# Past gates' sums at the down projection, a fixed order for TensorE in the mixer, prompt attention in rounds

## Chip, core and metric

The kernel runs on one core of a Trainium2 chip. The metric is the device time of one execution in microseconds (us). Engines: TensorE (PE; its weight loads are PEld), VectorE (DVE), ScalarE (ACT), GpSimd (POOL) and SyncE (SP). SP computes nothing here; it issues most DMAs, POOL issues the others, among them all indirect ones (gathers by an index).

## The reference

One step of a hybrid decoder layer, for a prompt of 1024 tokens and 8 samples of 4 new tokens, each with 2048 past tokens in pages of 128.

```
x = x + 0.5 * SwiGLU_1(RMSNorm(x))            # "up 1", "down 1"
p = RMSNorm(x) @ w_in                         # q | k | v | forget gates | B | C | u   ("mixer")
s[t,j] = q_t.k_j / 8 + sum of log f over (j,t]   # prompt, causal, 8 heads of 64
sample: the same over 16 gathered pages of k, v and log f, then the 4 new tokens
conv   = B * conv3(C * u)                     # 512 channels
x = x + w_out @ concat(RMSNorm(attn), RMSNorm(conv))
x = x + 0.5 * SwiGLU_2(RMSNorm(x));  final RMSNorm
suffix = lax.cumsum(lp, axis=1, reverse=True) - lp    # lp: the past log f, from the pages
```

All is float32. Each product of the projections is made of three matmuls (L102 to L104): weight and operand are split into a high part (a cast on ACT, L85 for weights, L191 for operands) and a remainder (a subtraction on DVE, L87 and L192).

## The kernel before

The 1056 tokens lie along the free axis, in four chunks of 264 for the feed-forward parts and in three of 352 for the mixer. The program is one stream of stages. For PE, ACT and DVE a scheduler sets the order within a stage; each engine then takes its instructions strictly in that order, and so do the queues of SP and POOL. A DMA is issued when its place in the queue has come and what it waits for is there.

**Up 1** (0 to about 480 us of the span) makes h = silu(.) * (.), and POOL stores it to h_d (L325, L330). **Down 1** (to about 747 us) takes h back: SP loads pieces of 128x528 (`h<-h_d`, L383), ACT and DVE split them (L191, L192), PE multiplies them with w2a (`ps<-h`). Eleven pieces are one chunk of tokens.

**Mixer** (to about 1160 us). First come the gates' logits and the first q tiles (`forget`, `proj`), then all of k, v, q and the convolution, 352 columns at a time (`pg<-XH`). Between them the samples' attention is dealt out as a generator A, 0.27 steps for each product: `sample_keys` gathers a page chunk `kvraw` (1 MB: two direct loads by SP, two gathers by POOL) and multiplies it (`sc`, L832), `sample_values` the same with v (`pv`, L880). What the past gates add comes from `load_gates`: 16 gathers of 64 KB (`R`, L598) for each group of four samples, which four scans on DVE (L823) sum into S. The indices `idl` are put in place by 16 small moves on SP (`by_pair`, L461). Weights of the mixer (`wraw<-in_w_in`) are loaded by SP too, in the same queue as the page chunks.

**Prompt attention** (1173 to 1327 us), 64 blocks of 128 queries, head by head. `logits` makes S (L1074, L1075, L1077), its maximum on DVE (L1079), the exponential on ACT (L1082), the sum's reciprocal and a scaling on DVE (L1083, L1084). `flip` transposes the probabilities (`ptp`, L1093) and copies them to PT (L1096); `weigh` makes O for two blocks at once (L1107), whose two halves ACT and DVE copy to `at`. `load_qk` (L1063) brings a head's KA, KB, QA, QB by eight loads on SP, `load_v` a pair's v. Two norms of the convolution's output (`conv_norm`: squares L140, `pco` L141, root L168, reciprocal L169, scaling L188, parts L191 and L192) are put after blocks 20 and 44. The order is set by `LA`, `PVD` and the scheduler:

```
LA, PVD, PTB, PRB = 3, 2, 5, 4
CONV_AT = (20, 44)
```

Then **w_out** (from 1327 us), **up 2** and **down 2**.

Of the kernel before, what the change touches and what calls it, by code (L numbers as in the profile page):

```python
# [8 lines left out]
F32 = mybir.dt.float32  # L9
# [9 lines left out]
P = 128  # L19
# [20 lines left out]
LA, PVD, PTB, PRB = 3, 2, 5, 4  # L40
RA = 0.27
CONV_AT = (20, 44)
# [384 lines left out]
def kernel(ctx: ExitStack, tc: tile.TileContext, io: dict):  # L427
# [34 lines left out]


# [8 lines left out]
    at_d = [dp.tile([P, TOK], F32, name=f"at_d{t}") for t in range(NHP)]  # L472
    qx_d = dp.tile([H, 4, SEQ], F32, name="qx_d")
# [64 lines left out]

    es_x = ExitStack()
    xpool = pool(es_x, "xh", "right")  # L540
    XH = xpool.tile([P, KD, TOK], F32R, name="XH")
# [26 lines left out]

    with ExitStack() as es:
        smp = pool(es, "smp", "left")  # L570
        mix = pool(es, "mix", "left")
# [4 lines left out]


        pt = mix.tile([P, NB * PAGES], I32, name="pt")
        nc.sync.dma_start(pt, io["pt"].rearrange("b s -> (b s)").rearrange("(o n) -> o n", o=1)
                          .broadcast_to([P, NB * PAGES]))  # L580
        ptl = mix.tile([P, 2, PAGES], I32, name="ptl")
        for b in range(NB):
            nc.sync.dma_start(ptl[32 * (b % 4):32 * (b % 4) + 32, b // 4, :],
                              io["pt"][b:b + 1, :].broadcast_to([32, PAGES]))
        cin = mix.tile([P, 2], I32, name="cin")
        nc.sync.dma_start(cin, io["cin"])
        idx = mix.tile([P, NB * PAGES], I32, name="idx")
        nc.vector.tensor_scalar(idx, pt, P, None, ALU.mult)
        nc.vector.tensor_tensor(idx, idx, cin[:, 0:1].broadcast_to([P, NB * PAGES]), ALU.add)
        ido = mix.tile([P, 2, PAGES], I32, name="ido")  # L590
        nc.vector.tensor_scalar(ido, ptl, H, None, ALU.mult)
        nc.vector.tensor_tensor(ido.rearrange("p g s -> p (g s)"), ido.rearrange("p g s -> p (g s)"),
                                cin[:, 1:2].broadcast_to([P, 2 * PAGES]), ALU.add)
        idl = mix.tile([P, 2, PAGES], I32, name="idl")
        by_pair(idl, lambda r: ido[r:r + 8])

        def gather(dst, src, ix):
            nc.gpsimd.indirect_dma_start(out=dst, out_offset=None, in_=src,  # L598
                                         in_offset=bass.IndirectOffsetOnAxis(ap=ix, axis=0))
# [189 lines left out]
        keys, new = [], []  # L789
# [9 lines left out]
        gates = {}  # L799

        def load_gates(g):

            gates[g] = []
            for i in range(4):
                R = smp.tile([P, 4, P], F32, tag="R", bufs=4, name="R")
                for s in range(4):
                    col = PAGES - 1 - (4 * i + s)
                    gather(R[:, s, :], io["lf"], idl[:, g, col:col + 1])
                gates[g].append(R)

# [5 lines left out]
        def sample_keys(g):  # L816

# [3 lines left out]
            for i, R in enumerate(gates[g]):  # L821
                n = 512 if i < 3 else 511
                nc.vector.tensor_tensor_scan(S[:, 512 * i + 1:512 * i + 1 + n],  # L823
                                             ones[:, 0:1].broadcast_to([P, n]),
                                             R.rearrange("p s k -> p (s k)")[:, :n],
                                             S[:, 512 * i:512 * i + 1], ALU.mult, ALU.add)
            for j in range(4):
                ps = psc.tile([P, 512], F32, tag="sc", name="sc")
                for b4 in range(4):
                    raw = kv_chunk()  # L830
                    for hp in range(NHP):
                        nc.tensor.matmul(ps[quarter(hp)], QZ[:, g, hp, 32 * b4:32 * b4 + 32],  # L832
                                         raw[:, :, hp * P:hp * P + P], start=b4 == 0, stop=b4 == 3)
                    if b4 < 3:
                        yield
                ks = slice(512 * j, 512 * j + 512)
                nc.vector.scalar_tensor_tensor(S[:, ks], ps, cq[:, g:g + 1], S[:, ks], ALU.add, ALU.add)
                yield
            pn = ptr.tile([P, 512], F32, tag="tr", name="pn")[:, :NS]
            if g == 0:  # L840
                load_gates(1)
            while not keys:
                yield
# [12 lines left out]
            yield  # L856
            PT = PTs[g] = smp.tile([P, PAGES + 1, P], F32, tag="PT", bufs=2, name="PT")
            for s0 in range(0, PAGES + 1, 4):
                n = min(4, PAGES + 1 - s0)
# [4 lines left out]
                if s0 == 4:  # L864
                    yield
            yield

        def sample_values(g):
            PT = PTs[g]
            while not new:  # L870
                yield

            pv = ppv.tile([P, 512], F32, tag="pv", name="pv")
            for b4 in range(4):
                cs = slice(P * b4, P * b4 + P)
                for j in range(4):
                    raw = kv_chunk()
                    for s in range(4):
                        for hp in range(NHP):
                            nc.tensor.matmul(pv[quarter(hp), cs], PT[:, 4 * j + s, quarter(hp)],  # L880
                                             raw[:, s, hp * P:hp * P + P], start=j == 0 and s == 0, stop=False)
                    if j < 3:
                        yield
                for hp in range(NHP):
                    nc.tensor.matmul(pv[quarter(hp), cs], PT[:, PAGES, quarter(hp)],
                                     new[0][:, hp * P:hp * P + P], start=False, stop=True)
                yield
            M = smp.tile([P, 512], F32, tag="M", bufs=1, name="M")
            nc.scalar.activation(M, pv, AF.Copy, scale=sums[g])
            po = ptr.tile([P, 512], F32, tag="tr", name="po")  # L890
# [9 lines left out]


        def vnew():
# [4 lines left out]
            new.append(VS)  # L907
# [51 lines left out]
        def values():  # L959
# [12 lines left out]
            vnew()  # L972
# [5 lines left out]
        def k_proj():  # L978
            for t in range(NHP):
                yield from proj(NHP + t, "k", t)  # L980
            keys.append(True)

        def q_rest():
            for t in range(1, NHP):
                yield from proj(t, "q", t, range(NMC - 1))

# [5 lines left out]
        load_gates(0)  # L992
# [3 lines left out]
        take(q0, 8)  # L996
        next(gate)
        take(q0, 5)
        next(gate)
        for t in range(1, NHP):  # L1000
            take(proj(t, "q", t, (NMC - 1,)), 5)
            next(gate, None)
# [17 lines left out]
    with ExitStack() as es:  # L1020
        ap_ = pool(es, "ap", "left")
        mix = pool(es, "mixb", "left")
        pco = pool(es, "pco", space=PSUM)
# [3 lines left out]
        RX = HD + 4  # L1027
        K.tmp = ap_
# [12 lines left out]
        def load_v(hp):  # L1041
            vt = ap_.tile([P, SEQ], F32, tag="vt", bufs=1, name="vt")
            nc.sync.dma_start(vt, v_d[hp])
            V = ap_.tile([P, 8, P], F32, tag="V", bufs=2, name="V")
            for j0 in range(0, 8, 4):
                pt_ = ptr.tile([P, 512], F32, tag="tr", bufs=2, name="ptv")
# [5 lines left out]

        def load_qk(h):

            hp, pr = h // 2, slice(HD * (h % 2), HD * (h % 2) + HD)
            KA, KB, QA, QB = (ap_.tile([P, SEQ], F32R, tag=n, bufs=2, name=n)
                              for n in ("KA", "KB", "QA", "QB"))
            (qh, ql), (kh, kl) = qk_d["q", hp], qk_d["k", hp]
            for dst, src in ((KA[:HD], kh[pr, :]), (KA[HD:], kh[pr, :]),
                             (QA[:HD], qh[pr, :]), (QA[HD:], ql[pr, :]),  # L1060
                             (KB[:HD], kl[pr, :]), (KB[HD:RX], kx_d[h]),
                             (QB[:HD], qh[pr, :]), (QB[HD:RX], qx_d[h])):
                nc.sync.dma_start(dst.bitcast(F32), src)  # L1063
            return KA, KB, QA, QB
# [285 lines left out]
```

## Time and profile before

| | us |
|---|---|
| median of 3 runs (lowest, highest) | 2198.26 (2195.49, 2204.02) |
| the profiled execution, its own time | 2176.51 |
| its span | 2174.8 |
| PE busy | 2082.3 |
| DVE busy | 1344.5 |
| ACT busy | 874.5 |
| POOL busy | 265.8 |

A span is the time from the first to the last instruction. The profiled execution is 1% under the median. Times in us, of one instruction in ns. PEclk is the granted clock of PE as a share of 2.4 GHz; 0.5 is its lower level, 1.2 GHz, and a mean between the two means that a stretch had some of both. A row of the timeline gives an instruction's start and duration, and in brackets how long its engine was idle before it and what ended that. `SPq` and `POOLq` are the engines' queues, in which the instructions that issue DMAs stand.

### The profile page before, as it was taken

Reading aid. Unit: us, or ns where it says so; the run is one execution under the profiler, and the core shown is the slowest. Engines: PE = TensorE matmul, PEld = TensorE weight load, DVE = VectorE, ACT = ScalarE, POOL = GpSimd, SP = SyncE. Lnnn points to the kernel's source line nnn. Section 1 sums busy time; section 2 is a strip of 40 time slices with the busy share of each in tenths; the row PEclk is TensorE's granted clock in tenths of the full one; section 3 lists DMA queues with packets and bytes.
Section 4 is the critical chain, followed back from the end, with each engine's and each line's share of the span. In section 5 each row is a group of like instructions: output and inputs, shape, how many; then the busy total and the mean of one; then the engine's idle time right before and its main releaser. Section 6 shows DMA issues by size and latency. Waiting matters only on the chain.

```text
span 2174.8 us, 44542 instructions
## 1 busy us (share of the span) xinstructions
PE 2082.3 (96%) x17570; PEld 1987.5 (91%) x17570; DVE 1344.5 (62%) x2586; ACT 874.5 (40%) x1738; POOL 265.8 (12%) x367
## 2 busy tenths in 40 slices
PE   7999999999999968899997999999999999999998
PEld 7999999999999856689996777989999999999997
DVE  8877777776656641132223785897667677775354
ACT  6533333345434421222112775454333333464343
POOL 0010011100000065323430000000110100100000
PEclk9999999999999988999997999999999999999999
DMA  6222223257545468887985545332222222496354
GB/s 210 79 96 84 84 87 98 85 178 237 178 154 203 157 183 271 305 289 234 281 255 149 125 102 166 133 114 84 89 77 72 86 87 84 136 321 202 108 177 132
DMA packets 139234, 336.84 MB, mean 155 GB/s; under 512 B 28192, under 2 KB 47616, under 8 KB 137488
## 3 DMA queue, kind: packets, MB, share of 16 engines
q1 hardware_dynamic: 117168, 265.23, 39.1%
q0 software_dynamic: 21856, 68.76, 9.0%
q8 instruction: 138, 2.26, 0.4%
q14 instruction: 72, 0.59, 0.1%
HBM read 277.66 MB, written 56.24 MB: 154 GB/s over the span
## 4 chain that ended last, share of the span: by engine, by line
PE 90%; DMA 4%; DVE 2%; ACT 1%; issue 1%; SPq 1%; POOL 1%; DVEq 0%; ACTq 0%; POOLq 0%
PE ps L104 23%; PE ps L103 23%; PE ps L102 23%; PE pg L102 4%; PE pg L103 4%; PE pg L104 4%; PE O L1107 2%; PE ptp L1093 1%; PE pv L880 1%; DMA wraw<-in_w_in 1%; PE sc L832 1%; PE S L1074 1%; PE ps L141 1%; PE S L1075 1%; DMA wraw<-in_w_out 1%
## 5 line engine op out<-in xcount | busy, mean ns | idle before, releaser
L104 PE MATMUL ps<-op,wl 128*128 128x264 f32 x2604 | 742.8, 286 | 0.0
L103 PE MATMUL ps<-op,wh 128*128 128x264 f32 x2604 | 741.1, 285 | 0.0
L102 PE MATMUL ps<-op,wh 128*128 128x264 f32 x2604 | 739.7, 285 | 1.3 <-ACT wh L85 0.9
L85 ACT CAST wh<-wraw 128x512 fp32r<-128x512 f32 x542 | 317.3, 600 | 497.2 <-PE ps L103 283.1
L87 DVE TENSOR_TENSOR wl<-wraw,wh 128x512 fp32r<-128x512 f32 x542 | 350.5, 662 | 232.5 <-ACT wh L85 208.0
L102 PEld LDWEIGHTS ps<-op,wh 128*128 128x128 f32 x2604 | 490.6, 189 | 2.1 <-ACT wh L85 1.1
L103 PEld LDWEIGHTS ps<-op,wh 128*128 128x128 f32 x2604 | 489.4, 188 | 0.5 <-DVE op L192 0.2
L104 PEld LDWEIGHTS ps<-op,wl 128*128 128x128 f32 x2604 | 489.6, 188 | 0.2
L102 PE MATMUL ps<-h,wh 128*128 128x264 f32 x1408 | 402.4, 286 | 0.0
L104 PE MATMUL ps<-h,wl 128*128 128x264 f32 x1408 | 398.7, 283 | 2.6 <-DVE wl L87 2.6
L103 PE MATMUL ps<-h,wh 128*128 128x264 f32 x1408 | 400.9, 285 | 0.0
L104 PEld LDWEIGHTS ps<-h,wl 128*128 128x128 f32 x1408 | 265.5, 189 | 2.8 <-DVE wl L87 2.8
L102 PEld LDWEIGHTS ps<-h,wh 128*128 128x128 f32 x1408 | 265.4, 188 | 0.2
L103 PEld LDWEIGHTS ps<-h,wh 128*128 128x128 f32 x1408 | 265.3, 188 | 0.2
L102 PE MATMUL pg<-XH,wh 128*128 128x352 f32 x576 | 193.0, 335 | 8.4 <-ACT wh L85 7.6
L103 PE MATMUL pg<-XL,wh 128*128 128x352 f32 x576 | 189.2, 329 | 0.0
L104 PE MATMUL pg<-XH,wl 128*128 128x352 f32 x576 | 187.7, 327 | 0.0
L85 ACT CAST wh<-s 128x512 fp32r<-128x512 f32 x176 | 108.1, 616 | 121.7 <-PE ps L103 110.4
L87 DVE TENSOR_TENSOR wl<-s,wh 128x512 fp32r<-128x512 f32 x176 | 120.5, 689 | 25.2 <-ACT wh L85 20.5
L102 PEld LDWEIGHTS pg<-XH,wh 128*128 128x128 f32 x576 | 110.9, 193 | 27.0 <-issue 13.2
L325 POOL DMA_DIRECT2D h_d<-t x79 | 42.6, 540 | 601.9 <-DVE t L324 601.9
L104 PEld LDWEIGHTS pg<-XH,wl 128*128 128x128 f32 x576 | 110.1, 191 | 0.9 <-DVE sm L854 0.8
(266 smaller groups left out, 2548.0 us busy)
## 6 DMA issues: line engine op xcount, KB each, us to landing
wraw<-in_w2a SPq DMA_DIRECT2D x48, 512.0 KB
wraw<-in_w2b SPq DMA_DIRECT2D x48, 512.0 KB
h_d<-t POOLq DMA_DIRECT2D x176, 132.0 KB, 2.0
h<-h_d SPq DMA_DIRECT2D x88, 264.0 KB
kvraw<-in_kc SPq DMA_DIRECT2D x64, 256.0 KB
kvraw<-in_vc SPq DMA_DIRECT2D x64, 256.0 KB
wraw<-in_w1a SPq DMA_DIRECT2D x28, 512.0 KB
wraw<-in_w3a SPq DMA_DIRECT2D x28, 512.0 KB
```

What stands on the lines that cost most here:

```text
L85: nc.scalar.copy(wh, x)
L87: nc.vector.tensor_sub(wl, x, wh)
L102: nc.tensor.matmul(ps, w[0], x[0], start=start, stop=False)
L103: nc.tensor.matmul(ps, w[0], x[1], start=False, stop=False)
L104: nc.tensor.matmul(ps, w[1], x[0], start=False, stop=stop)
L141: nc.tensor.matmul(ps, self.ones, sq, start=n == 0, stop=n == len(xs) - 1)
L325: nc.gpsimd.dma_start(h_d[2 * p + 1][:, f, :], t)
L832: nc.tensor.matmul(ps[quarter(hp)], QZ[:, g, hp, 32 * b4:32 * b4 + 32], raw[:, :, hp * P:hp * P + P], start=b4 == 0, stop=b4 == 3)
L880: nc.tensor.matmul(pv[quarter(hp), cs], PT[:, 4 * j + s, quarter(hp)], raw[:, s, hp * P:hp * P + P], start=j == 0 and s == 0, stop=False)
L1074: nc.tensor.matmul(S[:, k0:k1], QA[:, qs], KA[:, k0:k1], start=True, stop=False)
L1075: nc.tensor.matmul(S[:, k0:k1], QB[:RX, qs], KB[:RX, k0:k1], start=False, stop=not last)
L1107: nc.tensor.matmul(O[HD * b + q:HD * b + q + 32], V[:, j, c0 + q:c0 + q + 32], pt[:, j, :], start=j == 0, stop=j == n)
```

## The change

Four things change together.

1. **The past gates' sums** leave the mixer. The page indices, the 32 gathers R and the eight scans (now into a buffer B) are written between up 1 and down 1, and eight stores put the sums into a new tensor `bs_d` in memory. The mixer loads S from there (`new_sums`).
2. **TensorE's order in the mixer** is fixed by hand. The samples' work is a list of steps, `key_pages`, `new_keys`, `turn`, `value_pages`, `keep`, that `sample` deals out at a rate RA = 0.265 between the products. There are six page buffers instead of five, and five chunks are fetched while the gates' logits are made.
3. **Prompt attention in rounds.** A round is two blocks. For each round PE makes S of the next round, the transposes of this one and O of the one before, in an order fixed by hand. Both convolution norms stand after round 9; the transposing tiles have three PSUM buffers instead of two, shared with `pco`.
4. **Operands on POOL's queue.** `load_qk`, v and the stores of `at` are issued by POOL; the first head's operands already when the samples' steps are used up, during the last products of the convolution.

```diff
-LA, PVD, PTB, PRB = 3, 2, 5, 4
-RA = 0.27
-CONV_AT = (20, 44)
+RX = HD + 4
+PTB, PRB = 4, 4
+RA = 0.265
+CONV_AT = 9
...
     es_l.close()
     es_r.close()
+    es_x = ExitStack()
     xpool = pool(es_x, "xh", "right")
+    pt = xpool.tile([P, NB * PAGES], I32, name="pt")
+    idx = xpool.tile([P, NB * PAGES], I32, name="idx")
+    with ExitStack() as es:
+        gp = pool(es, "gp", "left")
...
+        idl = gp.tile([P, 2, PAGES], I32, name="idl")
+        by_pair(idl, lambda r: ido[r:r + 8])
+        for g in range(2):
+            last = None
+            for i in range(4):
+                R = gp.tile([P, 4, P], F32, tag="R", bufs=2, name="R")
+                for s in range(4):
+                    col = PAGES - 1 - (4 * i + s)
+                    gather(R[:, s, :], io["lf"], idl[:, g, col:col + 1])
+                B = gp.tile([P, 512], F32, tag="B", bufs=2, name="B")
+                nc.vector.tensor_tensor_scan(B, ones[:, 0:1].broadcast_to([P, 512]),
+                                             R.rearrange("p s k -> p (s k)"),
+                                             last if i else 0.0, ALU.mult, ALU.add)
+                last = B[:, 511:512]
+                n = 512 if i < 3 else 511
+                nc.sync.dma_start(bs_d[g][:, 512 * i + 1:512 * i + 1 + n], B[:, :n])
...
-            raw = smp.tile([P, 4, 512], F32, tag="kvraw", bufs=5, name="kvraw")
+            raw = smp.tile([P, 4, 512], F32, tag="kvraw", bufs=6, name="kvraw")
...
-            while len(raws) < min(n + 4, len(chunks)):
+            while len(raws) < min(n + 6, len(chunks)):
...
+        def new_sums(g):
             S = smp.tile([P, PAST + P], F32, tag="S", bufs=1, name="S")
             nc.gpsimd.memset(S[:, PAST + NS:], NEG)
             nc.vector.memset(S[:, 0:1], 0.0)
...
+            nc.sync.dma_start(S[:, 1:PAST], bs_d[g][:, 1:PAST])
+            Ss[g] = S
...
-        load_gates(0)
         gate = forget()
         q0 = proj(0, "q", 0)
         next(gate)
         take(q0, 8)
+        fetch()
...
-        A = chain(sample_keys(0), sample_keys(1), sample_values(0), sample_values(1))
-        due = 0.0
-        for _ in chain(k_proj(), values(), q_rest(), conv(range(4))):
-            due += RA
-            if due >= 2:
-                take(A, 2)
-                due -= 2
-        for _ in A:
-            pass
+        work = chain(k_proj(), values(), q_rest(), conv(range(4)))
+        for n, _ in enumerate(work):
+            sample(2 * int(RA * n / 2))
+            if not steps:
+                break
+        es_s.close()
+        es_a = ExitStack()
+        ap_ = pool(es_a, "ap", "left")
+        qk = {0: load_qk(0)}
+        for n, _ in enumerate(work):
+            if n == 5:
+                keep(1)
...
-                nc.sync.dma_start(dst.bitcast(F32), src)
+                nc.gpsimd.dma_start(dst.bitcast(F32), src)
...
-                copy = nc.vector.tensor_copy if h % 2 and j0 else nc.scalar.copy
+                copy = nc.vector.tensor_copy if i % 2 and j0 else nc.scalar.copy
...
-            nc.sync.dma_start(at_d[h // 2][vc, 256 * m:256 * m + 256], at[vc])
+            nc.gpsimd.dma_start(at_d[h // 2][vc, 256 * m:256 * m + 256], at[vc])
...
+        front(0)
+        for r in range(len(rounds)):
+            front(r + 1)
+            middle(r)
+            back(r - 1)
+            if r == CONV_AT:
+                for c in range(NCH // 2):
+                    conv_norm(c, K.tmp.tile([P, 4, CH], F32, tag="co", bufs=1, name="co"),
+                              ptr.tile([P, 512], F32, tag="tr", bufs=3, name="pco")[:, :CH])
+        back(len(rounds) - 1)
```

In `front(r)` the two calls of `logits` are made, for the first round of a head `load_qk` of the next head, and for every second head the load of v; `middle(r)` flips both blocks and turns v; `back(r)` calls `weigh`.

Three places show how the instructions move (line numbers after the change are one more up to the new code, so L383 is L384). The first is SP's queue where up 1 ends and down 1 begins; `in_w2a` are weights of down 1, `h` its operand. Before:

```order
L77 DMA wraw<-in_w3a 128x1024
L77 DMA wraw<-in_w2a 128x1024 x2
L77 DMA wraw<-in_w2a 128x768
L383 DMA h<-h_d_81 128x528 x11
L77 DMA wraw<-in_w2a 128x1024 x2
L77 DMA wraw<-in_w2a 128x768
```

and after the change, behind the same first weights and the moves of the page indices:

```order
L802 ISA x2
L582 DMA bs_d_117<-B 128x512 x3
L582 DMA bs_d_117<-B 128x511
L582 DMA bs_d_118<-B 128x512 x3
L582 DMA bs_d_118<-B 128x511
L384 DMA h<-h_d_81 128x528 x11
L593 DMA x<-in_xT 128x2112
L78 DMA wraw<-in_w2a 128x1024 x2
```

The eleven loads of h stand behind the eight stores of the sums. The second place is DVE at the same point; `s`, `u`, `m` and `t` are the gate products of up 1. Before:

```order
L307 TENSOR_TENSOR s_6244<-ps,m_6229 128x264
L192 TENSOR_TENSOR h<-h 128x528
L87 TENSOR_TENSOR wl<-wraw,wh 128x512
L311 TENSOR_TENSOR u_6260<-ps,m_6229 128x264
L192 TENSOR_TENSOR h<-h 128x528
L87 TENSOR_TENSOR wl<-wraw,wh 128x512
L192 TENSOR_TENSOR h<-h 128x528
```

and after, where L577 is the scan and R what POOL gathers:

```order
L330 TENSOR_TENSOR t<-t,s_6246 128x264
L561 TENSOR_SCALAR idx<-pt 128x128
L562 ISA idx<-cin,idx 128x256
L577 SCALAR_TENSOR_TENSOR B<-ones,R 128x512
L577 SCALAR_TENSOR_TENSOR B<-ones,B,R 128x512 x3
L577 SCALAR_TENSOR_TENSOR B<-ones,R 128x512
L577 SCALAR_TENSOR_TENSOR B<-ones,B,R 128x512 x3
L193 TENSOR_TENSOR h<-h 128x528 x11
```

The splitting of h stands behind the scans; PE's order at this place is the same in both. The third place is PE in the attention where the convolution's squares are summed. Before, such rows stand among others, here one by itself:

```order
L1048 MATMUL ptv<-cst,vt 128x128 x8
L1093 MATMUL ptp<-cst,Pr 128x128
L141 MATMUL pco<-sq,ones 128x264
L1093 MATMUL ptp<-cst,Pr 128x128 x5
L1074 MATMUL S<-KA,QA 128x512
```

and after:

```order
L1131 MATMUL ptp<-cst,Pr 128x128 x7
L1145 MATMUL O<-PT,V 32x128 x6
L142 MATMUL pco<-sq,ones 128x264 x8
L1112 MATMUL S<-KA,QA 128x512
L1113 MATMUL S<-KB,QB 128x512
```

The eight matmuls of both norms now follow one another.

## Rows read from the trace of the kernel before

**Rows 1.** The page: busy time of each engine.

```profile
PE 2082.3 (96%) x17570; PEld 1987.5 (91%) x17570; DVE 1344.5 (62%) x2586; ACT 874.5 (40%) x1738; POOL 265.8 (12%) x367
```

**Rows 2.** Stretches: us, busy PE PEld DVE ACT POOL, PEclk, DMA share, GB/s.

```profile
480.00:500.00 20.00, 20.00 (x167) 20.00 (x166) 14.49 (x28) 10.17 (x21) 1.08 (x2) 1.00 0.97 345
792.00:832.00 40.00, 18.35 (x91) 10.12 (x90) 6.52 (x9) 3.01 (x6) 30.52 (x33) 0.66 0.72 234
832.00:870.00 38.00, 33.37 (x195) 27.54 (x194) 6.90 (x13) 8.38 (x18) 15.04 (x16) 0.91 0.84 282
870.00:908.00 38.00, 31.50 (x191) 22.95 (x193) 8.47 (x14) 6.81 (x13) 12.65 (x15) 0.91 0.85 276
950.00:1000.00 50.00, 50.00 (x336) 40.95 (x336) 12.58 (x19) 9.27 (x18) 21.11 (x22) 1.00 0.94 322
1174.00:1190.00 16.00, 13.13 (x58) 9.81 (x58) 7.14 (x17) 7.52 (x21) 0.00 (x0) 0.54 0.69 176
1173.00:1327.00 154.00, 142.53 (x1748) 108.58 (x1749) 111.67 (x252) 107.48 (x265) 0.00 (x0) 0.94 0.45 108
```

**Rows 3.** Chain of waits, mixer's front: start, us, what.

```profile
813.26 5.23 DMA R<-in_lf,idl
...
840.15 8.86 DMA wraw<-in_w_in
```

**Rows 4.** Waits of PE ahead of the attention: total, times, longest.

```profile
PE S L1074 <- DMA QA<-q_d: 13.0, 1, 13.0
```

**Rows 5.** Chain of waits after the attention.

```profile
1335.43 6.06 DMA wraw<-in_w_out
...
1359.10 3.52 DMA wraw<-in_w_out
```

**Rows 6.** Timeline of SP, ACT, DVE and POOL where down 1 begins.

```profile
461.06 15.47 SPq L383 DMA_DIRECT2D h<-h_d  x11
...
471.94 0.63 ACT L191 CAST h<-h 128x528 fp32r<-128x528 f32 x1
...
473.15 0.70 DVE L192 TENSOR_TENSOR h<-h 128x528 fp32r<-128x528 f32 x1
...
474.37 0.42 DVE L311 TENSOR_TENSOR u<-ps,m 128x264 f32<-128x264 f32 x1
...
482.73 0.54 POOL L330 DMA_DIRECT2D h_d<-t  x1 [0.76 <-DVE t L329]
```

**Rows 7.** SP's index moves; tile R: its scans, and its landings.

```profile
762.01 10.85 SPq L461 DMA_DIRECT2D idl<-ido  x16
...
L823 DVE TENSOR_TENSOR_SCAN S<-ones,S,R x8: 1281/1284/1286, 790.5 to 930.0; 128x512 f32<-128x512 f32 x6, 128x511 f32<-128x511 f32 x2
...
DMA to landing us min/median/max: 2.5/3.3/5.2
```

**Rows 8.** Timeline of POOL, one of 27 such gathers.

```profile
776.36 0.94 POOL L598 DMA_INDIRECT R<-in_lf,idl  x1 [0.31 <-issue]
```

**Rows 9.** Groups by line in the attention: busy, mean ns, idle before.

```profile
L1093 PE MATMUL ptp<-cst,Pr 128*128 128x128 f32 x288 | 48.3, 285 | 2.9 <-ACT PT L1096 2.1 <-DVE PT L1096 0.8
```

**Rows 10.** The same view: the convolution's norms.

```profile
L169 DVE RECIPROCAL rs<-rs 128x264 f32<-128x264 f32 x2 | 3.6, 1798 | 0.4 <-ACT rs L168 0.4
L188 DVE SCALAR_TENSOR_TENSOR co<-co,prm,rs 128x264 f32<-128x264 f32 x8 | 3.5, 486 | 0.1
...
L140 ACT ACTIVATE sq<-co 128x264 f32<-128x264 f32 x8 | 3.2, 425 | 3.0 <-DMA co<-co_d 3.0
...
L168 ACT ACT_TABLE_LOAD x2 | 2.6, 1283 | 0.0
...
L192 DVE TENSOR_TENSOR opc<-co,opc 128x1056 fp32r<-128x1056 f32 x2 | 2.5, 1256 | 0.0
...
L191 ACT CAST opc<-co 128x1056 fp32r<-128x1056 f32 x2 | 2.1, 1074 | 0.7 <-DVE co L188 0.7
...
L168 ACT ACTIVATE rs<-pco,eps 128x264 f32<-128x264 f32 x2 | 1.0, 480 | 0.0
```

More of the change, by code (lines that the diff above doesn't have):

```diff
@@ L472 @@
     at_d = [dp.tile([P, TOK], F32, name=f"at_d{t}") for t in range(NHP)]
+    bs_d = [dp.tile([P, PAST], F32, name=f"bs_d{g}") for g in range(2)]
     qx_d = dp.tile([H, 4, SEQ], F32, name="qx_d")
@@ L797, in kv_chunk @@
             return raws[n]
[L799 to L809, printed above, removed]
         def quarter(hp):
@@ L820, in sample_keys, with key_pages, new_keys @@
             nc.vector.memset(S[:, 0:1], 0.0)
[L821 to L836, printed above, removed]
+            nc.sync.dma_start(S[:, 1:PAST], bs_d[g][:, 1:PAST])
+            Ss[g] = S
+        Ss, pss_, pvs = {}, {}, {}
+        def key_pages(g, j, b4):
+            if b4 == 0:
+                pss_[g] = psc.tile([P, 512], F32, tag="sc", name="sc")
+            ps, raw = pss_[g], kv_chunk()
+            for hp in range(NHP):
+                nc.tensor.matmul(ps[quarter(hp)], QZ[:, g, hp, 32 * b4:32 * b4 + 32],
+                                 raw[:, :, hp * P:hp * P + P], start=b4 == 0, stop=b4 == 3)
+            if b4 == 3:
+                ks, S = slice(512 * j, 512 * j + 512), Ss[g]
                 nc.vector.scalar_tensor_tensor(S[:, ks], ps, cq[:, g:g + 1], S[:, ks], ALU.add, ALU.add)
-                yield
+        def new_keys(g):
+            S = Ss[g]
             pn = ptr.tile([P, 512], F32, tag="tr", name="pn")[:, :NS]
[L840 to L843, printed above, removed]
             QN = smp.tile([P, NHP, 32], F32, tag="QN", bufs=1, name="QN")
@@ L863, in sample_keys, with value_pages, keep @@
                 nc.scalar.copy(PT[:, s0:s0 + n].rearrange("p s r -> p (s r)"), pt_[:, :n * P])
[L864 to L883, printed above, removed]
+            if b > PAGES and g == 0:
+                new_sums(1)
+        def value_pages(g, b4, j):
+            if b4 + j == 0:
+                pvs[g] = ppv.tile([P, 512], F32, tag="pv", name="pv")
+            PT, pv, raw = PTs[g], pvs[g], kv_chunk()
+            cs = slice(P * b4, P * b4 + P)
+            for s in range(4):
+                for hp in range(NHP):
+                    nc.tensor.matmul(pv[quarter(hp), cs], PT[:, 4 * j + s, quarter(hp)],
+                                     raw[:, s, hp * P:hp * P + P], start=j == 0 and s == 0, stop=False)
+            if j == 3:
                 for hp in range(NHP):
                     nc.tensor.matmul(pv[quarter(hp), cs], PT[:, PAGES, quarter(hp)],
[L886 to L890, printed above, removed]
+                                     VS[:, hp * P:hp * P + P], start=False, stop=True)
+            if b4 + j == 6:
+                Ms[g] = mix.tile([P, 512], F32, tag="M", bufs=1, name="M")
+                nc.scalar.activation(Ms[g], pv, AF.Copy, scale=sums[g])
+        Ms = {}
+        def keep(g):
+            po, M = ptr.tile([P, 512], F32, tag="tr", name="po"), Ms[g]
             for b4 in range(4):
@@ L1020 @@
     with ExitStack() as es:
-        ap_ = pool(es, "ap", "left")
-        mix = pool(es, "mixb", "left")
-        pco = pool(es, "pco", space=PSUM)
+        es.enter_context(tc.manual_schedule(engines={nc.tensor.engine}))
         ptr = pool(es, "ptr2", space=PSUM)
@@ L1126, in behind @@
-        def behind(k):
-            if k >= 0 and k % 2:
-                h, i = blocks[k]
-                weigh(h, i // 2, [pts.pop(k - 1), pts.pop(k)])
-        qk[0] = load_qk(0)
-        for n in range(LA):
-            ahead(n)
-        for n, (h, i) in enumerate(blocks):
-            ahead(n + LA)
-            pts[n] = ap_.tile([P, 8, P], F32, tag="PT", bufs=PTB, name="PT")
-            flip(h, i, prs.pop(n), pts[n])
-            behind(n - PVD)
-            if n in CONV_AT:
-                conv_norm(CONV_AT.index(n), ap_.tile([P, 4, CH], F32, tag="co", bufs=1, name="co"),
-                          pco.tile([P, 512], F32, tag="pco", bufs=1, name="pco")[:, :CH])
@@ L1142, with front @@
-        for k in range(len(blocks) - PVD, len(blocks)):
-            behind(k)
+            nc.gpsimd.dma_start(at_d[h // 2][vc, 256 * m:256 * m + 256], at[vc])
+        vs, prs, pts = {}, {}, {}
+        rounds = [(h, m) for h in range(H) for m in range(4)]
+        def front(r):
+            if r < len(rounds):
+                h, m = rounds[r]
+                prs[r] = [logits(h, 2 * m + b) for b in range(2)]
+                if m == 0 and h + 1 < H:
+                    qk[h + 1] = load_qk(h + 1)
+                if m == 0 and h % 2 == 0:
+                    vt = ap_.tile([P, SEQ], F32, tag="vt", bufs=1, name="vt")
+                    nc.gpsimd.dma_start(vt, v_d[h // 2])
+                    vs[h // 2] = vt
@@ new lines, in middle, with back @@
+        def middle(r):
+            h, m = rounds[r]
+            pts[r] = [ap_.tile([P, 8, P], F32, tag="PT", bufs=PTB, name="PT") for _ in range(2)]
+            for b, Pr in enumerate(prs.pop(r)):
+                flip(h, 2 * m + b, Pr, pts[r][b])
+            if m == 0 and h % 2 == 0:
+                vs[h // 2] = turn_v(vs[h // 2])
+        def back(r):
+            if r >= 0:
+                h, m = rounds[r]
+                weigh(h, m, pts.pop(r))
+        front(0)
[7 more added lines that the diff above has]
+                              ptr.tile([P, 512], F32, tag="tr", bufs=3, name="pco")[:, :CH])
```

133 lines of the change are left out of this document (74 added, 59 removed).

## The prediction

> **What bounds the kernel now.** I read the page first: TensorE (PE) is busy 96% of the span [rows 1]. So nothing can be won by freeing another engine; time is won only where PE stands still, or runs at the lower clock, and lost wherever the change makes it stand. The table of stretches shows where that is. The down projection at 480 us runs without a gap, at full clock, with the DMA engines 97% taken [rows 2]. The mixer's front, 792 to 908 us, does not: 116 us hold 83 us of busy PE, part of it below full clock. By 950 us PE is full. Behind the wait that ends at 1174 us it runs 16 us at a mean granted clock of 0.54. The prompt attention, 1173 to 1327 us, has PE busy 142.5 of 154 us at 0.94 [rows 2]. The chain of waits, read last, says what ended the idle time: POOL's gathers of the gates and their landings at 813 us, a weight piece queued behind page loads at 840 us and two more by 901 [rows 3], 13 us for the first QA tile ahead of the attention [rows 4], three pieces of w_out from 1335 to 1363 us behind it [rows 5].
>
> The sum is made on the profiled execution (2176.5 us; its span is 2174.8). The median of the timed runs is 2198.3, 1.0% above it, so I carry the difference over as a share.
>
> **1. The gates' sums, moved to the start of down 1: a new stall.** The change puts 16 small index moves (idl), 32 gathers (R), eight scans and eight stores (bs_d) between up 1 and down 1. What counts is what they stand ahead of. On SyncE (SP) the eight stores bs_d<-B now stand directly ahead of the eleven h loads; on VectorE (DVE) the eight scans stand ahead of all eleven `h<-h` subtractions, which before are interleaved with the last gate products of up 1. PE's own order there is the same as before: its next matmul is `ps<-h` and it cannot start without h. Before, SP issues the h loads from 461.06 us, under up 1's last matmuls, DVE's first h is at 473.15 us [rows 6], and PE goes from one projection to the other without a break: 20.00 of 20 us busy from 480 us [rows 2]. That cover goes.
>
> When does h come now? The index arithmetic sits on DVE behind the product that before starts at 474.37 us, so idl starts at about 476. In the row of before 16 such moves take SP 10.85 us: 487; landing takes the 2.5 us that is the least seen for a gather: 489.5 [rows 7]. By then POOL has issued the last h_d store (482.73 us [rows 6]), so the gathers start at once. One takes 0.94 us, the next starts 1.25 us after it [rows 8]: 32 x 1.25 = 40 us, to 529.5. The last is issued 1.25 us before that and lands 3.3 us after its issue (the median): 531.5. A scan is 1.28 us [rows 7], an issue on SP about 0.4: 533.2. Then an h load, 2.5 us, a cast on ScalarE (ACT) of 0.63 and a subtraction of 0.70 [rows 6]: PE restarts at 537 instead of 480. **Stall 57 us.**
>
> Two small things follow. Behind the h loads stand the x load and the weights of the second output tile: 11 x 0.27 + 1.08 + 0.52 MB at the 345 GB/s of [rows 2] is 13.2 us, while PE has 66 matmuls at the 167 in 20 us of that stretch (7.9 us) and 1.3 us of start: 4 us. And PE restarts from a long idle; the restart at 1174 us cost 16 us at 0.54, about 6 us [rows 2], part of which falls into waits for h here: 3 us. Together **+64 us**. The ends: 50 if the index moves take half as long and the tail overlaps, 76 if the two R buffers make gathers wait for landings of 5.2 us [rows 7].
>
> The gathers of before overlap: they start 1.25 us apart and land 3.3 us after their issue [rows 7, 8]. The Trainium skill prices one by itself: "DMA: Bandwidth & Descriptors", section "Anatomy of one DMA — SWDGE (gpsimd) path", gives a DMA from GpSimd about 2.0 us plus its bytes at 436 GB/s. By that a 64 KB gather is 2.15 us, and 32 one after the other would be 69 us, this term +93. I go by the rows; the other stays as a rival.
>
> **2. The mixer's front without the gates.** POOL's 32 gathers no longer stand ahead of the page gathers, six page buffers instead of five are used, and five chunks are fetched during the gate phase. What is lost today: busy time times clock is 18.35 x 0.66 + 33.37 x 0.91 + 31.50 x 0.91 = 71 us of work in 116 us, so 45 us [rows 2]. What remains: these 116 us move 40 x 0.234 + 38 x 0.282 + 38 x 0.276 = 30.6 MB. Away go 2.1 MB of gates and 5.2 MB fetched early; 23.3 MB at the 322 GB/s of the stretch 950 to 1000 us is 72 us, against 71 of work. DMA then only just follows, and the weight pieces still queue behind page loads on SP [rows 3], so I leave 8 us lost: **-37 us**, between -45 and -20 (the lower gain if no more goes than about half of what is lost: the 16 gathers of the second half of the gates, 20 us at 1.25 [rows 8], which stand between page gathers).
>
> **3. The gap before the attention.** The first head's operands are loaded by POOL during the last convolution work instead of after it, so the wait of 13.0 us for QA [rows 4] goes: **-13 us**, -9 to -16. What is late next is the last convolution product itself.
>
> **4. The attention in rounds.** Walking the measured durations [rows 9, 10] through both orders gives four parts. (a) Both convolution norms now stand in one place: eight pco matmuls in a row, where before other work lies between them. `co` has one buffer, so between the fourth and the fifth pco PE waits for the whole first norm: table load 1.28, root 0.48, reciprocal 1.80, four scalings 4 x 0.49, cast 1.07, subtraction 1.26, next co load about 3.5 (the rows show a 3.0 wait for one), a square 0.43: 11.8 us. After it the exponentials of the next round stand behind another table load and are late by some 6. The two norms cost before at most the 8 us of their squares and tables on ACT. Net +10. (b) vt for the first V is issued on POOL behind eight operand loads of head 1, and PE's order reaches ptv early: +4. (c) Rounds of two blocks: 16.5 to 18.0 us per head against 16.5, over eight heads 0 to +12, taken +4. (d) no half clock at the start: -4 of the 6 above. **+14 us.** The lower end: PE's work at full clock is 142.5 x 0.94 = 134 us of 154 [rows 2]; were all 20 lost us recovered save the norm stall of 12, this is -8. The upper end is +24.
>
> **5. After the attention.** SP no longer issues the operands, so w_out's pieces are there early; the three waits, 6.06 us the first and 3.52 the last [rows 5], shrink, but PE has other work under most of them, so I take about the larger one: **-5 us**, -3 to -7.
>
> **Sum:** +64 - 37 - 13 + 14 - 5 = +23 us, 1.06%. On the median of 2198.3: **2221 us**.
>
> **The rivals.**
> *The gates are covered (the other side).* If the h loads went ahead of the gates after all, or PE had other work, term 1 would be near 0 and the rest, -41, remains: 2198.3 x (1 - 41/2176.5) = 2157. It decides at a stall of 41 us: below that the kernel gets faster. For it: gathers need little of DMA, POOL is idle at 483 us. Against it: the order on SP, DVE and PE leaves no other way to h; half as many gathers would still leave some 37 us.
> *The rounds win time.* Three transposing PSUM buffers instead of two, and a whole round between S and its transposes, may bring PE to its work alone; then term 4 is -8 and the total +1: 2199. For it: PE waits today on copies and reductions between blocks, in many small pieces [rows 9]. Against it: the norm stall, which the order fixes.
> *The front stays bound by DMA.* If page loads and gathers get no more than the 282 GB/s of 832 to 870 us, 23.3 MB take 83 us, and with queueing of weights behind them the gain is 18: total +42: 2241. For it: DMA is 94% taken at 322 GB/s already at 950 us, with PE full [rows 2]. Against it: five chunks in hand.
> *Gathers one after the other.* If each gather began only when the one before had landed, 2.5 us at the least [rows 7], 32 would take 80 us instead of 40: total +63, 2262. Against it: POOL starts one every 1.25 us [rows 8], with landings of 3.3. The rule of the Trainium skill told under term 1 is this rival's; by its price the time would be 2251.
>
> **How the numbers follow.** Forecast 0.62, rounds 0.13, DMA-bound front 0.12, gates covered 0.08, serial gathers 0.05. Around the forecast the terms' ends, taken as independent, give +-20. The range from 2193 to 2243 takes in the rounds and the DMA-bound front, and leaves out the covered gates, the serial gathers and a small tail. A measurement of this kernel tells 0.5%, 11 us, from no change: slower than 2209 holds most of the forecast (0.57) and both slow rivals: 0.74; between 2187 and 2209: 0.16; faster: 0.10.
>
> **What would show it.** In the trace of the changed kernel: PE idle for 50 to 65 us before the first `ps<-h`, released by h and behind it the last bs_d and R; R gathers 1.25 us apart with nothing else on POOL; the front of the mixer with PE over 90% busy and no wait for R; no QA wait; the longest wait in the attention, some 12 us, at the fifth pco; w_out waits shorter. The prediction is wrong if PE's idle time at down 1 is under 40 us, or if the mixer's front still loses more than 20.

## The result, and the profile after

The changed kernel takes 2214.73 us (median of 4 runs, 2214.43 to 2216.04), the kernel before beside it 2198.85: a ratio of 1.0071, 95% interval 1.0051 to 1.0092. It is slower, as forecast, and the time lies in the range. In a later measurement (E9 below) the changed kernel takes 2213.78 us, as here, but the kernel before 2176.99: 1.0170 (1.0153 to 1.0187).

The two profiled executions differ by 2213.2 - 2174.8 = 38.4 us of span. The starts of the first and last instructions of a kind cut the span into stages; down 1 runs from the first `ps<-h` to the first `pg<-XH,wf`, the mixer to the last `pg<-XH`, the attention from the first S to the last O.

| stage, us | before | after | difference | forecast |
|---|---|---|---|---|
| up 1, to the first `ps<-h` | 479.9 | 538.8 | +58.9 | +57 |
| down 1 | 264.8 | 271.0 | +6.2 | +7 |
| mixer | 415.2 | 382.1 | -33.1 | -37 |
| gap ahead of the attention | 13.7 | 1.0 | -12.7 | -13 |
| attention | 152.7 | 174.2 | +21.5 | +14 |
| after it | 848.5 | 846.1 | -2.4 | -5 |
| span | 2174.8 | 2213.2 | +38.4 | +23 |

The waits of PE in the changed kernel (total, times, longest, in us) name the places:

```profile
PE ps L103 <- ACT h L192: 58.7, 1, 58.7
PE ptv L1099 <- DMA vt<-v_d: 14.5, 1, 14.5
PE pg L103 <- ACT wh L86: 12.6, 2, 9.5
...
PE pco L142 <- ACT sq L141: 10.3, 2, 9.5
```

The first stands where PE had no wait at all before. Around it, columns as in [rows 2]:

```profile
470.00:490.00 20.00, 10.16 (x84) 9.95 (x82) 8.51 (x20) 4.30 (x9) 2.45 (x5) 0.81 0.10 32
490.00:550.00 60.00, 10.57 (x66) 10.06 (x66) 17.80 (x20) 6.86 (x11) 30.50 (x32) 0.55 0.48 166
```

PE does 10.57 us of work in 60, at a mean granted clock of 0.55, near the lower level of 1.2 GHz. What runs there is in the timelines of SP, POOL and DVE, the rows that answer to [rows 6] to [rows 8]:

```profile
475.89 10.17 SPq L462 DMA_DIRECT2D idl<-ido  x15
...
497.77 35.48 SPq L582 DMA_DIRECT2D bs_d<-B  x8
533.87 5.74 SPq L384 DMA_DIRECT2D h<-h_d  x11
...
489.70 1.02 POOL L465 DMA_INDIRECT R<-in_lf,idl  x1 [7.77 <-DMA pt<-in_pt]
491.03 0.98 POOL L465 DMA_INDIRECT R<-in_lf,idl  x1 [0.30 <-issue]
...
529.00 0.94 POOL L465 DMA_INDIRECT R<-in_lf,idl  x1 [0.30 <-issue]
...
531.62 1.28 DVE L577 TENSOR_TENSOR_SCAN B<-ones,B,R 128x512 f32<-128x512 f32 x1 [3.68 <-DMA R<-in_lf,idl]
```

The index moves go out from 475.89 us, the 32 gathers follow from 489.70 to 529.00, most of them 1.25 us apart, the last scan begins at 531.62, SP issues the first h at 533.87, and the first `ps<-h` is at 538.8.

In the mixer's front PE is full from 882 us on, and the DMA engines move 338 and 354 GB/s there, where the highest mixer stretch of [rows 2] has 322:

```profile
809.00:870.00 61.00, 51.36 (x301) 44.58 (x301) 29.68 (x69) 19.52 (x48) 16.83 (x18) 0.93 0.72 231
870.00:882.00 12.00, 6.92 (x34) 6.18 (x38) 1.60 (x3) 2.41 (x5) 0.00 (x0) 0.66 0.69 239
882.00:950.00 68.00, 68.00 (x460) 55.25 (x453) 17.45 (x31) 15.94 (x33) 29.38 (x30) 1.00 0.98 338
950.00:1000.00 50.00, 49.67 (x331) 40.75 (x330) 9.19 (x19) 13.18 (x25) 19.73 (x21) 1.00 1.01 354
```

What is left lies ahead of that: PE works 58 of the 73 us from 809 to 882, the longest wait in it 9.5 us for a weight (`wh`). The 116 us of [rows 2] from 792 to 908 begin 47 us into the mixer; the same 116 us are here:

```profile
857.00:973.00 116.00, 106.17 (x697) 86.89 (x696) 23.59 (x44) 27.91 (x54) 42.06 (x44) 0.96 0.93 322
```

PE is busy 92% of them. Busy time times clock is 102 us, so 14 us are lost where the kernel before loses 45, and no wait of PE in the mixer is for R.

### The profile page after: what moved, and what is told of

It is laid out like the page before. It is cut to its first block, busy times and chain, and to the rows that moved or that the text cites. A ratio compares the mean times of both kernels' runs of the same rounds, so it can differ in the third digit from the quotient of the medians.

```text
span 2213.2 us, 44598 instructions
## 1 busy us (share of the span) xinstructions
PE 2070.6 (94%) x17570; PEld 1985.6 (90%) x17570; DVE 1351.2 (61%) x2586; ACT 869.2 (39%) x1736; POOL 318.4 (14%) x467
## 4 chain that ended last, share of the span: by engine, by line
PE 89%; DMA 3%; DVE 2%; issue 2%; ACT 1%; POOL 1%; SPq 1%; DVEq 0%; POOLq 0%; ACTq 0%
PE ps L104 23%; PE ps L105 23%; PE ps L103 23%; PE pg L103 4%; PE pg L105 4%; PE pg L104 4%; PE O L1145 2%; PE sc L839 1%; PE pv L882 1%; PE ptp L1131 1%; POOL R L465 1%; PE S L1112 1%; PE ps L142 1%; PE S L1113 1%; DMA vt<-v_d 1%
## 5 line engine op out<-in xcount | busy, mean ns | idle before, releaser
L103 PE MATMUL ps<-h,wh 128*128 128x264 f32 x1408 | 403.5, 287 | 60.2 <-ACT h L192 58.7
L103 PEld LDWEIGHTS ps<-h,wh 128*128 128x128 f32 x1408 | 266.2, 189 | 60.8 <-ACT h L192 58.9
```

The source lines that it names most:

```text
L103: nc.tensor.matmul(ps, w[0], x[0], start=start, stop=False)
```

## The experiments

The ratios are to the kernel before, run beside them on the same chip; on these four chips it took 2174.5 (E1 to E4), 2176.8 (E5 to E8), 2177.0 (E9 to E11) and 2178.6 us (E12).

**E1: the kernel before once more.** No edit.

> The kernel before, unchanged, profiled once more. The traces of the two kernels differ by 38 us, the medians by 16; the profiled execution of before was 22 us under its median. If executions of before differ in the mixer's front, where page loads, gathers and weights compete, this profile has another span there (792 to 908 us longer or shorter by some 20 us) and the same times elsewhere. If the 22 us are spread over the program (a clock, a chip), every stage is longer by about 1%. Ratio 1.000 in either case.

Measured: 2176.8 us; ratio 1.0007 (0.9994 to 1.0019). Its profile repeats the one of [rows 1]: down 1 263.0, mixer 411.5, attention 154.1, span 2170.8. So the executions of this kernel agree here, and none takes the 2199 us of the first measurement, of which there is no profile of the kernel before. Where it lost 22 us there stays open.

**E2: the stores of the sums on POOL's queue**, in the changed kernel.

```diff
-                nc.sync.dma_start(bs_d[g][:, 512 * i + 1:512 * i + 1 + n], B[:, :n])
+                nc.gpsimd.dma_start(bs_d[g][:, 512 * i + 1:512 * i + 1 + n], B[:, :n])
```

> The changed kernel with one edit: the eight stores bs_d<-B are issued by POOL, so that no store stands ahead of the h loads on SP. Theory 1 (three links hold h back: SP's order, the scans ahead of the subtractions on DVE, and the memory of R and B that h takes over): PE still waits 55 to 59 us at down 1, time as the changed kernel's, 2215. Rival: SP's queue alone holds h back; then the wait falls to a few us and the time to about 2157.

Measured: 2217.0 us (1.018); PE waits 62.7 us for the first h. SP's queue alone is not the cause. The waits of SP's queue, 480 to 545 us, show what the h loads (L384) then stand for:

```profile
SPq L384 <- DMA R<-in_lf,idl: 43.2, 2, 34.9
...
SPq L384 <- DVE B L577: 1.0, 1, 1.0
```

With no store ahead of them they wait for the gathers themselves: h takes over the memory in which R and B lie. Whether the scans on DVE alone would have held h back was not tried apart.

**E3: the gates dealt out over down 1.** R becomes a tile of one page in memory of its own, all DMAs go to POOL, and at each of the 32 output tiles stands:

```diff
+    def hook(n):
+        if n:
+            gate_sum(n - 1)     # a scan of 128 columns in place, a store
+        gate_row(n)             # one gather
```

> The changed kernel with the gates' work dealt out over the 32 output tiles of down 1: at each one gather of one page, one scan of 128 columns and one store, all DMAs on POOL, R and B one small tile in memory that h does not use. Theory 1 (the stall is the whole cost of moving the gates, and they need little of DVE, POOL and DMA): PE's wait of 58.7 us goes, the mixer is as in the changed kernel, time 2215 - 62 = 2153. Rival (work beside down 1 costs as much there, since DVE is busy and waits in order for gathers): 2190 or more, with PE waiting for wl or h in many places.

Measured: 2218.2 us (1.0195). The rival is right. The one wait of 58.7 us is gone, but down 1 takes 330.1 us. PE now waits in many places (total, times, longest):

```profile
PE ps L105 <- DVE wl L88: 27.0, 11, 5.8
PE ps L104 <- DVE h L193: 17.5, 4, 14.4
```

The groups by line of DVE in that stage (busy, mean ns, idle before and what ended it):

```profile
L88 DVE TENSOR_TENSOR wl<-wraw,wh 128x256 fp32r<-128x256 f32 (+1 forms) x142 | 85.6, 637 | 22.9 <-ACT wh L86 21.2 <-PE ps L104 1.6
...
L583 DVE TENSOR_TENSOR_SCAN R<-ones,R 128x128 f32<-128x128 f32 x32 | 15.3, 480 | 99.5 <-DMA R<-in_lf,idl 67.4 <-issue 32.1
```

The scans cost 15.3 us of work and 99.5 us of standing: the scheduler had moved each of them ahead on DVE, to a place where its rows had not landed, and behind it stood the weights' subtractions for which PE waits. The last of the 32 scans begins at 683.5 us, 125 us ahead of the stage's end. One stall of 59 us had become many smaller ones.

**E4: only the gates moved, in the kernel before**, dealt out as in E3; the mixer's S is loaded from `bs_d`.

> The kernel before with only the gates moved, in the dealt-out form; mixer, its order, five page buffers, and attention as before. If the gates' gathers on POOL were what the mixer's front lost (theory 1), the front gains 25 to 40 us: 2160 to 2174 on the median of before. If the front is bound by DMA and weights behind page loads (rival), the gain is under 15 us: 2184 or more.

Measured: 2201.9 us (1.0113). The time lies where the rival put it, but not for the rival's reason: down 1 stands as in E3 (338.4 us). The mixer, read by itself, takes 375.0 us against 415.2 and 411.5 before: moving the gates and their page indices, with nothing else, gives its whole gain.

**E5: each scan tied behind a later sum**, else E3; the gather, too, is now written behind the tile's last sum.

```diff
-                    nc.vector.scalar_tensor_tensor(x, o, 0.5, x, ALU.mult, ALU.add)
+                    added = nc.vector.scalar_tensor_tensor(x, o, 0.5, x, ALU.mult, ALU.add).ins
+                    if hook and c == cs[-1]:
+                        hook(KD * n + d, added)
...
+        with tc.issue_after(added):
+            if n:
+                gate_sum(n - 1)
```

> The dealt-out gates with each scan tied on DVE behind the sum of the next output tile, some 8 us after its gather was issued, so that DVE never reaches a scan whose rows have not landed. In the earlier dealt-out kernel DVE sat 99 us before its scans, and down 1 took 330 us instead of 265. Theory 1 (the price of the gates beside down 1 is only the waiting of an engine that works in order): down 1 takes 265 to 270 us, time 2215 - 60 = 2155. Rival (32 gathers and stores among the loads of h and weights slow these): down 1 still takes over 285 us, time over 2175.

Measured: 2163.7 us, 0.9947 (0.9929 to 0.9965): 50 us below the changed kernel. Down 1 takes 278.9 us, between the two expectations. The same row of DVE:

```profile
L583 DVE TENSOR_TENSOR_SCAN R<-ones,R 128x128 f32<-128x128 f32 x31 | 14.8, 476 | 36.9 <-DMA R<-in_lf,idl 18.7 <-issue 17.9 <-DVE x L407 0.4
```

Its idle time fell from 99.5 to 36.9 us, and with it the stage, by 51. Down 1 still takes 14 us more than in the kernel before (264.8).

**E6: v first.** In the changed kernel `vt` of the first pair is loaded behind the operands of head 0.

```diff
         qk = {0: load_qk(0)}
+        load_v(0)
```

> The changed kernel; v of the first pair of heads is loaded by POOL right behind the operands of head 0, ahead of the convolution's stores and head 1's operands. Theory 1 (the wait of 14.5 us for vt is POOL's queue: vt is issued at 1198.6 us, behind a wait for the store out_cso and eight loads): the wait goes, 2215 - 12 = 2203. Rival (the next late thing takes its place, the first rounds' exponentials or head 1's operands): 2209 or more.

Measured: 2203.0 us (1.0136). The attention takes 164.4 us instead of 174.2, and no wait for vt is left. POOL's timeline in the changed kernel shows where vt had stood:

```profile
1182.33 0.91 POOL L953 DMA_DIRECT2D out_cso<-E  x1
...
1192.36 0.53 POOL L917 DMA_DIRECT2D KA<-k_d  x1 [2.51 <-DMA out_cso<-E]
...
1198.61 0.58 POOL L1164 DMA_DIRECT2D vt<-v_d  x1 [1.06 <-DMA KA<-k_d]
1214.27 0.54 POOL L1164 DMA_DIRECT2D vt<-v_d  x1 [15.08 <-PE ptv L1099]
```

The store out_cso was issued at 1182.33 us; the second load of KA waits for its landing until 1192.36, and vt, the last of these loads, for that KA until 1198.61. (The row behind it is the load for the second pair, which waits for PE's ptv.) The chain puts 9.74 us on the store, 5.97 on that KA and 13.35 on vt's own transfer, which takes 3.7 to 4.0 us for each pair in E6. Meanwhile, 1198 to 1212 us, PE does nothing and the DMA engines are 97% taken by head 1's operands, x and w_out:

```profile
1198.00:1212.00 14.00, 0.00 (x0) 0.00 (x1) 3.90 (x8) 4.56 (x12) 0.58 (x1) 0.50 0.97 266
```

**E7: the norms apart**, in the changed kernel.

```diff
-CONV_AT = 9
+CONV_AT = (9, 21)
...
-            if r == CONV_AT:
-                for c in range(NCH // 2):
+            if r in CONV_AT:
+                for c in [CONV_AT.index(r)]:
```

> The changed kernel with the two convolution norms put behind rounds 9 and 21 instead of both behind round 9. Theory 1 (10 us of waiting at the fifth pco come from one co buffer with both norms in one place, and about 4 more from the exponentials behind them): 2215 - 10 = 2205, with no wait over 3 us at pco. Rival (a norm costs its own time on ACT and DVE wherever it stands): 2211 or more, two waits of 5 us or more.

Measured: 2200.1 us (1.0107). The attention takes 162.0 us, and the waits at pco fell from 10.3 to 1.8 us:

```profile
PE ptv L1099 <- DMA vt<-v_d: 13.8, 1, 13.8
PE ptp L1131 <- DVE Pr L1122: 5.2, 8, 0.8
...
PE pco L142 <- ACT sq L141: 1.8, 2, 1.0
```

**E8: E5, E6 and E7 together.**

> The tied gates, the early v and the norms apart together. If the three are independent: 2155 - 12 - 10 = 2133, faster than before by about 2%. If they hide behind one another, 2150 or more.

Measured: 2144.4 us, 0.9854 (0.9831 to 0.9878), faster than both kernels. Read in their own stages the gains add up: down 1 ends 49.4 us earlier than in the changed kernel (52.0 in E5), and the attention takes 153.2 us, 21.0 less (9.8 and 12.2 in E6 and E7) and as in the kernel before (152.7). The 2133 expected were too low, because E5 was taken with 60 us.

**E9: the changed kernel once more.** No edit.

> The changed kernel, unchanged, beside the kernel before on this chip. The kernel before took 2199 us in the first measurement and 2175 and 2177 in the two later ones, the changed kernel 2215 in the first. If the changed kernel differs between chips as the kernel before does, it takes some 2190 here and the ratio stays 1.007. If only the kernel before does, it takes 2215 and the ratio is 1.018 where before takes 2175.

Measured: 2213.8 us (2211.9 to 2216.6), ratio 1.0170. Only the kernel before differs between the measurements.

**E10: only the gates moved, tied, in the kernel before.**

> The kernel before with only the gates moved, now with each scan tied behind a later sum as in the kernel that took 2164. Theory 1 (the gates' gathers and indices are what the mixer's front lost; moved without a stall they give 35 us, and down 1 pays some 8): 2175 - 27 = 2148. Rival (the fixed order of PE and the sixth page buffer give most of the mixer's gain): 2165 or more.

Measured: 2160.9 us, 0.9929 (0.9912 to 0.9946). The time is nearer to the rival, the stages are not: the mixer takes 383.8 us (-31.4) with PE's order, five page buffers and the gap as before, and down 1 281.1 us (+16.3) where I had allowed 8. For fixed order, sixth buffer and the early fetch in the code 1.7 us are left, between 383.8 and 382.1. That is no gain that these runs show: the same mixer code took 375.0 us in E4. POOL's timeline says why the gates suffice (the kernel before first, then E10):

```profile
763.84 0.99 POOL L598 DMA_INDIRECT kvraw<-in_kc,idx  x1 [0.30 <-issue]
...
797.88 0.95 POOL L598 DMA_INDIRECT kvraw<-in_kc,idx  x1 [0.30 <-issue]
...
770.68 1.00 POOL L467 DMA_INDIRECT kvraw<-in_kc,idx  x1 [0.17 <-issue]
...
782.12 1.02 POOL L467 DMA_INDIRECT kvraw<-in_kc,idx  x1 [0.30 <-issue]
```

Before, two page gathers are issued, then 16 of R, and the third page gather at 797.88. In E10 ten page gathers follow one another from 770.68 to 782.12: five chunks, all five buffers, ahead of the front, without a fetch written for it. The indices are made earlier, too; what they alone are worth was not tried apart.

**E11: weights one projection ahead**, in E8.

```diff
             for t in range(NHP):
-                yield from proj(NHP + t, "k", t)
+                ahead = K.load(io["w_in"][NHP + t + 1], D) if t + 1 < NHP else None
+                yield from proj(NHP + t, "k", t, raw=raw)
+                raw = ahead
```

> The kernel with all three edits, and each k projection's weights loaded one projection ahead, so that the load of k1's weights stands ahead of the page loads on SP instead of behind them. In the kernel with all three PE waits once 9.3 us for these weights, the longest wait left in the mixer. If the order on SP is its cause: that wait goes, 2144 - 9 = 2135. If DMA is simply taken there (0.76 of its time), the wait moves to a page: 2142 or more.

Measured: 2148.0 us, 0.9865 (0.9848 to 0.9881): no gain over E8. The mixer takes 382.4 us against 382.1. The wait at k1 is gone, but one for the next weights that were not loaded ahead, those of the first v, comes some 45 us later. Waits of PE from 860 to 900 us, and stretches:

```profile
PE pg L103 <- ACT wh L86: 11.6, 1, 11.6
...
835.00:850.00 15.00, 15.00 (x102) 11.68 (x101) 3.83 (x7) 3.93 (x8) 5.52 (x6) 1.00 1.00 350
850.00:862.00 12.00, 10.40 (x68) 8.45 (x67) 2.50 (x5) 2.82 (x6) 5.55 (x6) 1.00 1.01 344
862.00:880.00 18.00, 8.00 (x31) 7.78 (x32) 2.59 (x4) 2.73 (x5) 1.07 (x2) 0.62 0.68 244
```

and, of SP's timeline and the chain:

```profile
859.14 4.21 SPq L817 DMA_DIRECT2D kvraw<-in_kc  x4
...
865.25 6.05 DMA wraw<-in_w_in
```

The time is the rival's, but the wait moved to another weight and not to a page. PE stands from 860.4 to 872.0 us. The first 4.9 us of that pass while SP still issues page loads and stores that stand ahead of the weight, then 6.05 go to the weight's transfer and 0.63 to its cast. The DMA engines are wholly taken from 835 to 862 us, and at 0.68 behind that. So SP's order and the taken DMA engines both have a part by these rows, and the run does not separate them. That the pages, let ahead sooner, shift the wait to the next weight is argued, not shown.

**E12: the page indices made later**, in E8: two operations of DVE go from the start of down 1 behind its output tile number 12 (counted from 0).

> The kernel with all three edits, and the two small operations that make the page indices idx from pt moved on DVE from the start of down 1 behind its twelfth output tile. There DVE stood from 490 to 497 us for the landing of pt, with a sum and weight subtractions queued behind. Down 1 takes 280 us with the gates beside it and 265 without them. Theory (each of these 15 us is DVE standing before something of the gates that has not landed; idx is the first of them): PE gains 3 to 5 us around 495, 2144 - 4 = 2140. Rival (the loss is DMA and POOL traffic, not DVE's order): 2143 or more.

Measured: 2144.5 us, 0.9845 (0.9822 to 0.9869), as E8. PE gained at the place and lost behind it: 478 to 500 us hold 21.69 us of PE work instead of 19.37, 500 to 540 us 36.92 instead of 39.78. DVE's waits in down 1 say why (E8 first, then E12):

```profile
DVE R L583 <- issue: 16.3, 5, 4.1
DVE R L583 <- DMA R<-in_lf,idl: 14.9, 8, 3.4
...
DVE idx L566 <- DMA pt<-in_pt: 5.9, 1, 5.9
...
DVE R L581 <- DMA R<-in_lf,idl: 22.4, 10, 5.6
...
DVE R L581 <- issue: 15.8, 5, 4.2
```

The 5.9 us for pt are gone, and the scans stand 38.2 us instead of 31.2. The first scan became the next to wait: 5.6 us for its rows instead of 1.4. The time is the rival's, and what makes up the 14 to 16 us that down 1 pays for the gates beside it stays open.

## Why the prediction was right, point by point

**Term 1, the stall: right in size and in mechanism.** Forecast 57 us and 7 behind it; measured 58.9 and 6.2. Each step of the chain came within 2 us: first gather forecast at 489.5, seen at 489.70; last scan at 531.5 and 531.62; first h load at 533.2 and 533.87; PE at 537 and 538.8. Of the 6.2 us, the trace shows a clock of 0.50 for the first 4 us and a wait of 1.5 us for a weight. The rest is within what this stage differs by between two profiles of the changed kernel (271.0, and 268.9 in E9). Not foreseen was a third link, the memory that h takes over from R and B (E2): freeing SP's queue would not have helped. The rival "covered" needed the h loads ahead of the gates; E5 is such a kernel: the stall is gone, and it takes 2163.7 us where the rival had 2157.

The rival "one after the other" fails in POOL's rows, 1.25 us apart to the end. The estimate of 2.15 us for a 64 KB gather comes from the price of the Trainium skill ("DMA: Bandwidth & Descriptors", section "Anatomy of one DMA — SWDGE (gpsimd) path"), which is for one DMA; the section does not say that several follow one another. The shortest landing of [rows 7] is 2.5 us, and 32 in a row go out 1.25 us apart, so here they overlap.

**Term 2, the mixer's front: right in size, and for the first of its three reasons.** Forecast -37, measured -33.1; the front still loses 14 us where I had left 8. E10 gives -31.4 for the gates and their indices alone, and five chunks ahead come with them. The sixth buffer and the early fetch, which the sum counted beside the gates, show no gain of their own. The sum also took all 32 gathers out of the 116 us; in the kernel before 20 of them lie there, 1.3 MB and not 2.1. The DMA-bound rival took the page loads at 282 GB/s; they run at 338 and more with PE full. Whether DMA binds what the front still loses stays open (E11).

**Term 3: right,** -13 and -12.7. The wait for QA is gone, and POOL issues the first QA at 1152.70 us, 40 us ahead of the first S. E10 keeps a gap of 11.7 us, so it is not the gates that close it; the early operands were not tried by themselves.

**Term 4, the attention: the term that was mis-sized,** +14 forecast and +21.5 measured. Its part (b), the late vt, was put at 4 us from eight issues on POOL; it is a wait of 14.5 us, worth 9.8 in E6. I had counted what stands ahead of vt in POOL's queue, not what those entries wait for (the second KA waited for the store out_cso), nor that vt then shares DMA with all that SP and POOL have issued by then. So the longest wait of the attention is this one, and not that at the fifth pco, as forecast (9.5 us instead of some 12). Part (a), the norms in one place, was put at 10 us net; E7 gives 12.2 back. Parts (c) and (d), +4 and -4, were forecast to cancel, and they do: with vt early and the norms apart the attention takes 153.2 us against 152.7. The runs do not separate the two. The attention's first 16 us in E8 are

```profile
1143.00:1159.00 16.00, 12.76 (x71) 9.58 (x71) 11.73 (x25) 8.91 (x24) 5.45 (x10) 0.79 1.02 273
```

against 13.13 us at 0.54 in [rows 2]: busy time times clock is 10.1 instead of 7.1. So by estimate (d) gives 3 us, and the rounds (c) cost about as much. The rival, by which the rounds win time, is not borne out.

**Term 5:** -2.4 instead of -5. The three loads of [rows 5] are gone from the chain, but the gain is hardly larger than the 2.0 us by which two profiles of the kernel before differ in this stage (848.5, and 850.5 in E1).

**The total** was right partly by luck. The terms of the profiled executions sum to +38.4, not +23, since the attention (7.5 us), the mixer (3.9) and the rest (2.6) came out worse. What brought the time to 7 us of the forecast is the base: I carried the difference to a median of 2198, which the kernel before shows on none of the four later chips. Against 2177 there, the changed kernel is 36.8 us slower, and the change of 23 us that I forecast is too small by 14.

## What to carry to other kernels

Work that is moved beside a busy stage has to be read in the order of every in-order engine it touches: it costs nothing only if what it waits for has landed when the engine comes to it, and only if the next stage neither queues behind it nor takes over its memory. Dealing such work out in small pieces does not help by itself (E3: 99.5 us of standing on VectorE); tying each piece behind a later instruction did (E5: 50 us, with 14 us still paid beside down 1). And of a DMA that is put into another queue, count what the entries ahead of it wait for, not only how long they take to issue.

## What the runs showed of the hardware

- POOL issued 32 gathers of 64 KB with 1.25 us from one to the next, as in [rows 8], with nothing else on its queue and the DMA engines 29% taken (491 to 529 us). A gather lands 3.3 us after its issue [rows 7], so the pace here is that of the issue, not of the landing.
- Gathers and direct loads together moved 354 GB/s over 50 us (950 to 1000 us) with PE busy 49.67 of them; the kernel before moved 322 there.
- The kernel before took 2198.9 us in the first measurement and 2174.5 to 2178.6 on four chips later, the changed kernel 2214.7 and 2213.8. A difference of 1% that only one of two kernels shows was not expected, and its cause stays open.
